# Small tensors of a low-rank gate: loaded by another engine, prepared two products sooner

## The chip, the cores and the metric

The kernel runs on one core of one Trainium2 chip. Its time is the device time of one execution, in microseconds (us); a kernel is given by the median of several executions. The core has TensorE (PE in the profile: matrix products, with PEld for its weight loads), VectorE (DVE), ScalarE (ACT), GpSimd (POOL) and SyncE (SP, which in this kernel only issues DMAs). Each engine takes its instructions strictly in the order in which they were written down for it; an instruction that waits for a semaphore holds up all behind it on its engine.

## The reference

One layer of a hybrid decoder, 1024 tokens of width 1024, all in float32:

```python
h = rms_norm(x, pre_g)
z = einsum('bsd,de->bse', h, w_in)
qa, ka, va, ga, qb, kb, vb, gb, gk_low = split_columns(z)
...                                   # differential attention on qa, ka, va, gated by ga
gk = einsum('bsr,re->bse', gk_low, w_gk_up) + b_gk
log_a = log_sigmoid(gk) / 16
ob = gla_chunked(qb, kb, vb, log_a)   # gated linear attention
...
y = einsum('bse,ed->bsd', concatenate([oa, ob]), w_out)
return x + rms_norm(y, post_g)
```

The part that matters here is the low-rank gate: gk_low is a product of h with only 16 columns of w_in (a "low rank" of 16), and w_gk_up (16 x 512) widens it to the 512 gate values.

## The kernel before, in words

**Products.** The wide product h @ w_in is made by Strassen's method in Winograd's form: h and w_in are cut into 2 x 2 blocks, and seven block products replace eight. In the code a product is a pair (p, n): p a group of 256 columns of w_in (the list `pairs`; 0 to 3 are the values of the linear attention, 4 is the first of the attention's keys), n the number of the product, 1 to 7. The left factors are blocks or sums of blocks of h: h11, h12, h22, s1 to s4 (`LEFT`); the right ones blocks or differences of blocks of w_in. `order` lists all products in the order in which PE makes them. Around the change it runs: (0,5) (1,5) (0,6) (1,6) (0,4) (0,7) (1,4) (1,7), the first half of the low-rank product, (2,5), its second half, (3,5), (0,3) and so on. For pairs 0 to 3 one set of prepared weights serves both pairs of a couple: the weights of (0,6) are also those of (1,6).

**High and low parts.** To keep float32's precision, each factor is split into a high part, rounded to PE's fast format (fp32r), and a low part, the rest. A product is three matmul passes: high x high, high left x low weights, low left x high weights. So each weight costs a subtraction that forms the block difference (DVE, `w_raw<-w_raw`), a rounding (ACT, `CAST w<-w_raw`) and a second subtraction for the low part (DVE, `w<-w_raw,w`). The function `parts` does the same for a block of h: high part by ACT (`s_hi`, `h_hi`), low part by DVE (`s_lo`, `h_lo`); it returns the low part's instruction.

**Order of the work.** `go(n)` makes the next n products. Before product i it calls `prepare` for i to i + 3, and `make_weights` then writes down the operations of those weights and the loads of raw weights (`load_raw`, on SP). PE's order is that of the program, fixed by hand. The other engines' order comes from a planner that runs a model of the timeline while the kernel is built: whenever an engine comes free in the model, it takes the ready instruction that stands first in the program. So an instruction that the program names early has a higher rank, but one of lower rank that is ready earlier fills a hole. `tc.issue_after(ins)` adds an edge: the instructions within it that are for the engine of `ins` come behind `ins` in that engine's order.

**Blocks of h.** `blocks(j)`, for j = 0 to 3, transposes the lower rows of h, makes h21, h22 and the sums s1 = h21 + h22, s3 = h11 - h21 and s2 = s1 - h11, and splits them with `parts`. It returns the low parts of s2 and s3; after the last call they are in `behind`. They are used twice: `prepare` puts the weights of (0,4) behind the low part of s2 (L290), and the four sums s4 come behind both.

**Low-rank product.** `low_rank` (L783) clears `keep`, loads w_gk_up (16 x 512) into `gk_up` and the 16 columns of w_in into `wl` (1024 rows of 16 values, 64 bytes each), both by `sp.dma_start` (L790, L794), clears `wl2`, `gkl` and `up`, and then has DVE make, from `wl`, the block difference `wd`, and the high and low parts of both in `wl2`; and from `gk_up` the high and low parts in `up`. Then come `go(2)`, which is (1,4) and (1,7), and the two halves of the low-rank product, 16 matmuls each (`gkl_ps`): first the high, then the low parts of h against `wl2`. `gk_up`, `wl` with `wd`, and the tiles c, s1, h21 of other steps share a ring of four buffers, `t_c`. In the profile `wl2` is shown as wl, `up` and `keep` as ku.

Of the kernel before, what the change touches and what calls it, by code (L numbers as in the profile page):

```python
# [18 lines left out]
KT = D // P  # L19
HB = 4  # L20
# [5 lines left out]
QA, KA, VA, GA, QB, KB, VB, GB, GKL = 0, 1024, 2048, 3072, 4096, 4608, 5120, 6144, 7168  # L26
GK_RANK = 16
# [4 lines left out]
def hymba_kernel(  # L32
# [21 lines left out]
    pe, sp = nc.tensor, nc.sync  # L54
# [80 lines left out]
    def take_bank(shape, name):  # L135
        i = free.pop(0)
        return bank(i, shape, name), i
# [6 lines left out]
    def tr(dst, src):  # L144
        tc.keep_in_program_order(pe.transpose(dst, src, ident))  # L145
# [8 lines left out]
    def block(n):  # L154
        if n not in H:
            pool_h, pieces = (hpool, 1) if n in ("s3", "s4") else (hw, 2)
            H[n] = [
                [
                    pool_h.tile(
                        [P, HB // pieces, 512], F32R, tag=f"{n}_{part}{i}", name=f"{n}_{part}"  # L160
                    )
                    for i in range(pieces)
                ]
                for part in ("hi", "lo")
            ]
# [9 lines left out]
    kp = ctx.enter_context(tc.tile_pool(name="kp", bufs=1))  # L175
# [67 lines left out]
    order = [(0, 1), (1, 1), (0, 2), (1, 2), (2, 1), (3, 1), (2, 2), (3, 2), (4, 1), (4, 2)]  # L243
# [16 lines left out]
    i = order.index((1, 4))  # L260
# [22 lines left out]
    def prepare(i):  # L283

        if i >= len(order) or i in ws:
            return
        if 4 <= i <= n_early + 1:
            with tc.issue_after(act.last), tc.issue_after(dve.last):
                make_weights(i)
        elif order[i] == (0, 4):  # L290
            with tc.issue_after(behind[0].ins):
                make_weights(i)
        else:
            make_weights(i)
# [44 lines left out]
    def make_weights(i):  # L339
        p, n = order[i]  # L340
        if (wide(p) and p % 2) or p == VALS[1]:
            ws[i] = ws_wide[p - 1, n]
            return
        if p in VALS:
            ws[i] = ws_wide[p, n] = value_weights(n)
            return
        if p in early and n < 3:
            src = early[p][n - 1]
        else:
            fetch_raw(p, n, i)  # L350
# [12 lines left out]
            if n == 5:  # L363
                src = sub(b11, b12, b11)
            elif n == 6:
                src = sub(b11, b22, b11)
            elif n == 4:
                src = sub(b21, b21, b11)
            elif n == 7:
                src = sub(b12, b22, b12)  # L370
            else:
                src = {1: b11, 2: b21, 3: b22}[n]
        if wide(p):
            w = [ap.tile([P, HB, 256], F32R, tag="ring", name="w", bufs=NRING) for _ in range(2)]
# [299 lines left out]
    def parts(n, j, f):  # L674
        hi, lo = block(n)
        act.copy(at(hi, j), f)
        return dve.tensor_tensor(at(lo, j), f, fp(at(hi, j)), ALU.subtract)

    def blocks(j):


        pss = []
        for k in (j, j + HB):
            ps, i = take_bank([P, 512], "xT")
            for n in range(4):
# [12 lines left out]
        parts("h22", j, h22)  # L698
        parts("s1", j, s1)
        h11 = f1[0][:, j]  # L700
        dve.tensor_tensor(h21, h11, h21, ALU.subtract)
        dve.tensor_tensor(h11, s1, h11, ALU.subtract)
        return [parts("s2", j, h11), parts("s3", j, h21)]

    made = [0]
    fill = []
# [32 lines left out]
    def go(n):  # L739
        for _ in range(n):  # L740
            i = made[0]
            if i == len(order):
                return
            made[0] = i + 1
            for a in range(4):
                prepare(i + a)
            step(i)
            if order[i][0] >= EARLY and order[i][0] not in VALS:
                wo_step(order[i][1])
            for _ in range(2 if order[i][0] in VALS else 1):  # L750
                if fill and next(fill[0], 0) == 0:
                    fill.pop(0)
# [11 lines left out]
    for j in range(HB):  # L764
        behind = blocks(j)
# [14 lines left out]
    ku = kp.tile([P, 2, 512], F32R, tag="ks1", name="ku")  # L780
    up, keep = ku[:, 0], fp(ku)[:, 1]

    def low_rank():  # L783


        R = GK_RANK
        pool.memset(keep, 1.0)
        pool.memset(keep.rearrange("p (c i) -> p c i", i=64)[:, :, 0:1], 0.0)
        gk_up = t_c("gk_up")[:R]
        sp.dma_start(gk_up, w_gk_up[0])  # L790
        wl2 = kp.tile([P, KT + HB, 64], F32R, tag="q0", name="wl2")
        wd = t_c("wd").rearrange("p (k r) -> p k r", r=R)
        wd, wl = wd[:, KT : KT + HB], wd[:, :KT]
        sp.dma_start(wl, w_in[0, :, GKL : GKL + GK_RANK].rearrange("(k p) c -> p k c", p=P))  # L794
        pool.memset(fp(wl2), 0.0)
        dve.tensor_tensor(wd, wl[:, HB:], wl[:, :HB], ALU.subtract)
        for dst, src in ((wl2[:, :KT], wl), (wl2[:, KT:], wd)):
            dve.tensor_copy(dst[:, :, :R], src)
            dve.tensor_tensor(dst[:, :, 32 : 32 + R], src, fp(dst[:, :, :R]), ALU.subtract)
        pool.memset(fp(gkl), 0.0)  # L800
        pool.memset(fp(up), 0.0)
        dve.tensor_copy(up[0:R], gk_up)
        dve.tensor_copy(up[32 : 32 + R], gk_up)
        dve.tensor_tensor(up[64 : 64 + R], gk_up, fp(up[0:R]), ALU.subtract)
        dve.tensor_tensor(up[96 : 96 + R], gk_up, fp(up[0:R]), ALU.subtract)
        go(2)
        for half in range(2):
            cs = cols(half)
            ps, i = take_bank([P, 512], "gkl_ps")
            terms = ((0, "h11"), (HB, "h12")) if half == 0 else ((0, "s1"), (KT, "h22"))  # L810
            for part in range(2):
                for o, n in terms:
                    for k in range(HB):
                        mm(
                            ps[:64], wl2[:, o + k, :], at(H[n][part], k),
                            start=(part == 0 and o == 0 and k == 0),
                            stop=(part == 1 and o != 0 and k == HB - 1),
                        )
            free.append(i)
            low = t_c("low")[:R]  # L820
            act.copy(low, ps[32 : 32 + R])
            dve.tensor_tensor(low, low, ps[:R], ALU.add)
            dve.tensor_copy(gkl[0:R, cs], low)
            dve.tensor_copy(gkl[64 : 64 + R, cs], low)
            dve.tensor_tensor(gkl[32 : 32 + R, cs], low, fp(gkl[0:R, cs]), ALU.subtract)
            dve.tensor_tensor(gkl[96 : 96 + R, cs], low, fp(gkl[0:R, cs]), ALU.subtract)
            go(1)

    def decay(g):
# [27 lines left out]
        act.activation(b, b, AF.Exp, scale=1.0 / 16)  # L857
        decs[g] = b, t

    go(4)  # L860
    sp.dma_start(bgk, b_gk[0].rearrange("(t p) -> p t", p=P))
    low_rank()
# [814 lines left out]
```

## Time and profile before

| | |
|---|---|
| median of three runs | 976.76 us |
| the three runs | 976.76, 975.23, 977.49 us |
| the profiled execution | 977.06 us |
| its span, first to last instruction | 975.4 us |
| mean granted clock of PE | 0.997 |
| busy: PE, DVE, ACT, POOL | 960.7, 736.2, 604.3, 203.3 us |

The profile is that of one execution. Its time lies 1.7 us above its span. A row of a timeline has the start in us from the span's begin, the length in us (of several like instructions together), the engine (SPq is SP's queue), the line, the operation, what it writes and reads, and how many instructions; in brackets the idle time of the engine before it and whose end ended it. L66 is the helper through which most operations go, L142 the matmul helper, so a row is known by its tiles. A row of the waits names who waited for whom: us in total, how often, the longest. A row of the windows gives the stretch and then, for each engine, its busy time; PEclk is the clock that PE was granted, 1.00 being full speed.

### The profile page before, as it was taken

The page shows a single profiled execution, that of the slowest core. Times are in us where ns is not written, and L with a number is a line of the kernel's source. Part 1 is how long each engine was busy: PE and PEld are TensorE (multiplying, and loading weights), DVE is VectorE, ACT ScalarE, POOL GpSimd, SP SyncE. Part 2 cuts the span into 40 slices and gives each one's busy share as a digit, 9 for nine tenths or more (in the row PEclk, how much of TensorE's full clock was granted, in tenths as well). Part 3 has the DMA queues.
Part 4 walks back from the last instruction along what each step waited for, and adds up shares of the span by engine and source line. Part 5 has one row for each costly group of instructions (what it writes and reads, how often), then busy time and mean ns, then how long its engine had stood idle before and what let it go on. Part 6 is the DMA issues. An engine that isn't in the chain of part 4 may idle for free.

```text
span 975.4 us, 15092 instructions
## 1 busy us (share of the span) xinstructions
PE 960.7 (98%) x4977; PEld 815.6 (84%) x4977; DVE 736.2 (75%) x1464; ACT 604.3 (62%) x1166; POOL 203.3 (21%) x264
## 2 busy tenths in 40 slices
PE   9998999999999999999999999999999999999997
PEld 7997988888888888888888888878888888888785
DVE  5996598997677686686766576587888888898555
ACT  8741354664766555576765344366786777887773
POOL 4300001222141221221100002121322222443322
PEclk9999999999999999999999999999999999999999
DMA  9442357468668987996764589997656669994777
GB/s 359 149 124 76 119 152 253 163 224 302 219 195 259 279 278 264 286 285 216 249 190 146 167 245 283 390 289 244 225 177 218 234 198 349 327 297 104 152 206 149
DMA packets 152302, 220.39 MB, mean 226 GB/s; under 512 B 16753, under 2 KB 87409, under 8 KB 152129
## 3 DMA queue, kind: packets, MB, share of 16 engines
q1 hardware_dynamic: 138128, 178.80, 57.3%
q0 software_dynamic: 14096, 40.64, 14.4%
q8 instruction: 39, 0.64, 0.3%
q14 instruction: 39, 0.31, 0.1%
HBM read 133.93 MB, written 88.60 MB: 228 GB/s over the span
## 4 chain that ended last, share of the span: by engine, by line
PE 88%; DVE 4%; DMA 4%; SPq 2%; issue 2%; ACT 1%; POOL 0%; DVEq 0%; ACTq 0%; POOLq 0%
PE x L142 22%; PE z L142 15%; PE y L142 14%; PE ypart L142 12%; PE sc L142 6%; PE po L142 5%; PE yps L142 4%; PE wtr L145 3%; PE gpo L142 3%; PE kv L142 1%; DMA w_early<-in_w_in_dram 1%; PE gkl_ps L142 1%; DVE p L66 1%; DMA mixd<-gate 1%; PE pa L142 1%
## 5 line engine op out<-in xcount | busy, mean ns | idle before, releaser
L66 ACT CAST w<-w_raw 128x512 fp32r<-128x512 f32 (+1 forms) x150 | 98.0, 655 | 90.5 <-PE y L142 46.3
L66 DVE TENSOR_TENSOR w<-w_raw,w 128x512 fp32r<-128x512 f32 (+1 forms) x150 | 109.3, 731 | 50.4 <-ACT w L66 46.2
L66 ACT ACTIVATE p<-p,stt 128x896 f32<-128x896 f32 (+7 forms) x128 | 99.3, 777 | 36.2 <-DVE stt L66 35.2
L66 ACT COPY s<-x 128x512 f32<-128x512 f32 x82 | 47.7, 586 | 92.5 <-PE x L142 92.0
L66 POOL TENSOR_SCALAR p<-p,stt,lam 128x1024 f32<-128x1024 f32 (+3 forms) x64 | 56.0, 874 | 148.4 <-DVE stt L66 146.6
L66 POOL DMA_DIRECT2D wo_d<-wo_hi x32 | 17.6, 550 | 331.3 <-ACT wo_hi L66 331.3
L66 DVE CUSTOM_DVE_ANT_0 p<-sc,maskt 128x512 f32<-128x512 f32 (+3 forms) x128 | 74.2, 585 | 14.3 <-PE sc L142 13.1
L142 PE MATMUL z<-s_hi,w 128*128 128x512 f32 x320 | 80.2, 393 | 0.0
L142 PE MATMUL x<-s_hi,w 128*128 128x512 f32 x320 | 80.1, 392 | 0.0
L142 PE MATMUL y<-h_hi,w 128*128 128x512 f32 x320 | 80.0, 392 | 0.0
L142 PE MATMUL ypart<-wo_hi,m_hi 128*128 128x512 f32 x192 | 79.5, 414 | 0.1
L142 PE MATMUL ypart<-wo_hi,m_lo 128*128 128x512 f32 x192 | 75.5, 393 | 0.0
L142 PE MATMUL ypart<-wo_lo,m_hi 128*128 128x512 f32 x192 | 75.4, 393 | 0.0
L142 PE MATMUL sc<-k,q 128*128 128x512 f32 (+1 forms) x192 | 69.1, 363 | 1.7 <-DVE stt L66 1.7
L142 PEld LDWEIGHTS y<-h_hi,w 128*128 128x128 f32 x320 | 59.7, 188 | 12.3
L142 PEld LDWEIGHTS z<-s_hi,w 128*128 128x128 f32 x320 | 59.7, 188 | 12.3
L142 PEld LDWEIGHTS x<-s_hi,w 128*128 128x128 f32 x320 | 59.7, 188 | 12.3
L66 DVE TENSOR_TENSOR w_raw<-w_raw 128x512 f32<-128x512 f32 (+1 forms) x88 | 66.1, 751 | 3.3 <-DMA w_raw<-in_w_in_dram 2.2
L142 PE MATMUL sc<-ks,q 128*128 128x512 f32 (+1 forms) x192 | 66.1, 347 | 0.0
L66 ACT CAST wt_hi<-wtr 128x512 fp32r<-128x512 f32 (+1 forms) x80 | 42.7, 534 | 25.7 <-PE wtr L145 24.9
L66 DVE TENSOR_TENSOR wt_lo<-wtr,wt_hi 128x512 fp32r<-128x512 f32 (+1 forms) x80 | 50.6, 632 | 9.5 <-ACT wt_hi L66 8.8
L66 DVE TENSOR_TENSOR c<-z,s 128x512 f32<-128x512 f32 x48 | 32.9, 688 | 31.4 <-ACT s L66 18.3
(223 smaller groups left out, 2350.0 us busy)
## 6 DMA issues: line engine op xcount, KB each, us to landing
w_raw<-in_w_in_dram SPq DMA_DIRECT2D x48, 512.0 KB, 4.8
wo_d<-wo_hi POOLq DMA_DIRECT2D x32, 256.0 KB, 3.8
q<-q_d SPq DMA_DIRECT2D x32, 256.0 KB, 5.2
k<-k_d SPq DMA_DIRECT2D x32, 256.0 KB, 5.8
ks<-k_d SPq DMA_DIRECT2D x64, 128.0 KB, 6.2
v<-v_d SPq DMA_DIRECT2D x16, 512.0 KB, 7.7
wo_raw<-in_w_out_dram POOLq DMA_DIRECT2D x31, 256.0 KB, 4.9
wo_d<-gqd POOLq DMA_DIRECT2D x22, 256.0 KB, 4.3
```

The lines of the kernel that those rows point to most:

```text
L66: ins = op(*a, **k)
L142: tc.keep_in_program_order(pe.matmul(*a, **k))
L145: tc.keep_in_program_order(pe.transpose(dst, src, ident))
```

## The change

Two edits that are apart from each other, and a third that serves the first.

1. The low-rank gate's preparation becomes a function of its own, `low_rank_weights`. It is called after products (0,6) and (1,6), two products sooner in the program than before, and `low_rank` keeps only the two halves of the product. PE's order stays as it was: the two calls `go(2)` and `go(4)` cover the six products that `go(4)` and the inner `go(2)` covered.
2. Its two loads are issued by POOL, not SP; its DVE operations stand behind `behind[0]`, the low part of s2 of the last block.
3. `blocks` also returns the low part of s1, and the weights of (0,6) stand behind it (`behind[2]`). Before, only those of (0,4) stood behind anything.

```diff
@@ -287,8 +287,8 @@
-        elif order[i] == (0, 4):
-            with tc.issue_after(behind[0].ins):
+        elif order[i] in ((0, 6), (0, 4)):
+            with tc.issue_after(behind[2 if order[i] == (0, 6) else 0].ins):
                 make_weights(i)
@@ -696,11 +696,11 @@
-        parts("s1", j, s1)
+        s1_lo = parts("s1", j, s1)
...
-        return [parts("s2", j, h11), parts("s3", j, h21)]
+        return [parts("s2", j, h11), parts("s3", j, h21), s1_lo]
@@ -780,30 +780,33 @@
-    def low_rank():
-
-
-        R = GK_RANK
+    wl2 = kp.tile([P, KT + HB, 64], F32R, tag="q0", name="wl2")
+    R = GK_RANK
+
+    def low_rank_weights():
+
         pool.memset(keep, 1.0)
         pool.memset(keep.rearrange("p (c i) -> p c i", i=64)[:, :, 0:1], 0.0)
         gk_up = t_c("gk_up")[:R]
-        sp.dma_start(gk_up, w_gk_up[0])
-        wl2 = kp.tile([P, KT + HB, 64], F32R, tag="q0", name="wl2")
+        pool.dma_start(gk_up, w_gk_up[0])
         wd = t_c("wd").rearrange("p (k r) -> p k r", r=R)
         wd, wl = wd[:, KT : KT + HB], wd[:, :KT]
-        sp.dma_start(wl, w_in[0, :, GKL : GKL + GK_RANK].rearrange("(k p) c -> p k c", p=P))
+        pool.dma_start(wl, w_in[0, :, GKL : GKL + GK_RANK].rearrange("(k p) c -> p k c", p=P))
         pool.memset(fp(wl2), 0.0)
-        dve.tensor_tensor(wd, wl[:, HB:], wl[:, :HB], ALU.subtract)
-        for dst, src in ((wl2[:, :KT], wl), (wl2[:, KT:], wd)):
-            dve.tensor_copy(dst[:, :, :R], src)
-            dve.tensor_tensor(dst[:, :, 32 : 32 + R], src, fp(dst[:, :, :R]), ALU.subtract)
         pool.memset(fp(gkl), 0.0)
         pool.memset(fp(up), 0.0)
-        dve.tensor_copy(up[0:R], gk_up)
...
-        go(2)
+        with tc.issue_after(behind[0].ins):
+            dve.tensor_tensor(wd, wl[:, HB:], wl[:, :HB], ALU.subtract)
+            for dst, src in ((wl2[:, :KT], wl), (wl2[:, KT:], wd)):
+                dve.tensor_copy(dst[:, :, :R], src)
+                dve.tensor_tensor(dst[:, :, 32 : 32 + R], src, fp(dst[:, :, :R]), ALU.subtract)
+            dve.tensor_copy(up[0:R], gk_up)
...
+
+    def low_rank():
+
         for half in range(2):
@@ -857,6 +860,8 @@
+    go(2)
+    low_rank_weights()
     go(4)
     sp.dma_start(bgk, b_gk[0].rearrange("(t p) -> p t", p=P))
     low_rank()
```

More of the change, by code (lines that the diff above doesn't have):

```diff
@@ L789, in low_rank @@
         gk_up = t_c("gk_up")[:R]
-        sp.dma_start(gk_up, w_gk_up[0])
-        wl2 = kp.tile([P, KT + HB, 64], F32R, tag="q0", name="wl2")
+        pool.dma_start(gk_up, w_gk_up[0])
         wd = t_c("wd").rearrange("p (k r) -> p k r", r=R)
         wd, wl = wd[:, KT : KT + HB], wd[:, :KT]
-        sp.dma_start(wl, w_in[0, :, GKL : GKL + GK_RANK].rearrange("(k p) c -> p k c", p=P))
+        pool.dma_start(wl, w_in[0, :, GKL : GKL + GK_RANK].rearrange("(k p) c -> p k c", p=P))
         pool.memset(fp(wl2), 0.0)
-        dve.tensor_tensor(wd, wl[:, HB:], wl[:, :HB], ALU.subtract)
-        for dst, src in ((wl2[:, :KT], wl), (wl2[:, KT:], wd)):
-            dve.tensor_copy(dst[:, :, :R], src)
-            dve.tensor_tensor(dst[:, :, 32 : 32 + R], src, fp(dst[:, :, :R]), ALU.subtract)
         pool.memset(fp(gkl), 0.0)
         pool.memset(fp(up), 0.0)
-        dve.tensor_copy(up[0:R], gk_up)
-        dve.tensor_copy(up[32 : 32 + R], gk_up)
-        dve.tensor_tensor(up[64 : 64 + R], gk_up, fp(up[0:R]), ALU.subtract)
-        dve.tensor_tensor(up[96 : 96 + R], gk_up, fp(up[0:R]), ALU.subtract)
-        go(2)
+        with tc.issue_after(behind[0].ins):
[4 more added lines that the diff above has]
+            dve.tensor_copy(up[0:R], gk_up)
+            dve.tensor_copy(up[32 : 32 + R], gk_up)
+            dve.tensor_tensor(up[64 : 64 + R], gk_up, fp(up[0:R]), ALU.subtract)
+            dve.tensor_tensor(up[96 : 96 + R], gk_up, fp(up[0:R]), ALU.subtract)
+    def low_rank():
         for half in range(2):
```

## The prediction

> **What bounds the kernel now.** I read the page first, for which engine sets the time; then the list of what TensorE (PE) waited for; then the timeline of PE, to place these waits; then those of DVE, ACT and SP around them.
>
> ```profile
> PE 960.7 (98%) x4977; PEld 815.6 (84%) x4977; DVE 736.2 (75%) x1464; ACT 604.3 (62%) x1166; POOL 203.3 (21%) x264
> ...
> PE gkl_ps L142 <- DVE wl L66: 2.7, 1, 2.7
> PE z L142 <- DVE s_lo L66: 0.5, 1, 0.5
> ```
>
> PE is busy for 960.7 of 975.4 us, so only its few waits can be won. The two lines are both in the stage that the diff touches. PE's timeline there (start, length, idle time before it and who ended it):
>
> ```profile
> 52.87 0.50 PE L142 MATMUL z<-w,s_lo 128*128 128x256 f32 x2 [0.51 <-DVE s_lo L66]
> ...
> 56.09 2.08 PE L142 MATMUL x<-w,s_hi 128*128 128x256 f32 x16
> ...
> 61.85 2.08 PE L142 MATMUL y<-w,h_hi 128*128 128x256 f32 x16
> ...
> 72.41 1.12 PE L142 MATMUL x<-w,s_lo 128*128 128x256 f32 x8
> 76.27 3.27 PE L142 MATMUL gkl_ps<-h_hi,wl 128*64 128x512 f32 x8 [2.74 <-DVE wl L66]
> ...
> 81.22 2.08 PE L142 MATMUL z<-w,s_hi 128*128 128x256 f32 x16
> ...
> 84.09 1.07 PE L142 MATMUL gkl_ps<-s_hi,wl 128*64 128x512 f32 x4
> ...
> 87.76 2.08 PE L142 MATMUL z<-w,s_hi 128*128 128x256 f32 x16
> ```
>
> PE stood still for 0.51 us before 52.87, in the product (0, 5), which lacked the last low part of the sum s1; and for 2.74 us before 76.27, because the low-rank weights `wl2` (shown as wl) were not ready. The second stall costs more than its length. The 16 matmuls of the first low-rank half run from 76.27 to 81.22, 4.95 us; the 16 of the second, the same shapes, from 84.09 to 87.76, 3.67 us. The granted clock says why:
>
> ```profile
> 73.50:76.20 2.70, 0.03 (x1) 0.00 (x0) 2.70 (x5) 1.63 (x2) 0.00 (x0) 0.88 0.00 0
> 76.20:77.50 1.30, 1.24 (x3) 0.73 (x4) 1.30 (x3) 0.00 (x0) 0.00 (x0) 0.50 0.31 34
> ```
>
> The clock was at 0.50 right after the idle stretch: 4.95 - 3.67 = 1.28 us. So the two places hold 0.51 + 2.74 + 1.28 = 4.53 us, 0.46% of the span.
>
> The Trainium skill's page "TensorE: Matmul & The Clock Gate" (Part 1: The HAM clock gate) has the clock fall to half after an idle window of about 3.4 us; taken strictly, 2.74 us of idling would not do it, and the sum would lack the 1.28. The trace shows the drop after 2.74 us, and the trace decides.
>
> **Why wl was late.** It is no long operation; it stands at the end of two queues. SP's and DVE's rows:
>
> ```profile
> 58.72 5.05 SPq L220 DMA_DIRECT2D w_raw<-in_w_in_dram  x3
> 63.82 0.50 SPq L790 DMA_DIRECT2D gk_up<-in_w_gk_up_dram  x1
> 64.38 0.41 SPq L794 DMA_DIRECT2D wd<-in_w_in_dram  x1
> ...
> wd<-in_w_in_dram SPq DMA_DIRECT2D x1, 64.0 KB, 4.4
> ```
>
> ```profile
> 50.40 1.21 DVE L66 TENSOR_TENSOR w_raw<-w_raw 128x1024 f32<-128x1024 f32 x1
> 51.54 0.68 DVE L66 TENSOR_TENSOR h<-f1hi,h 128x512 f32<-128x512 f32 x1
> 52.14 0.68 DVE L66 TENSOR_TENSOR s_lo<-s,s_hi 128x512 fp32r<-128x512 f32 x1
> ...
> 54.54 1.21 DVE L66 TENSOR_TENSOR w<-w_raw,w 128x1024 fp32r<-128x1024 f32 x1
> ...
> 56.88 0.68 DVE L66 TENSOR_TENSOR s_lo<-f1hi,s_hi 128x512 fp32r<-128x512 f32 x1
> 57.49 1.21 DVE L66 TENSOR_TENSOR w_raw<-w_raw 128x1024 f32<-128x1024 f32 x1
> 58.62 2.48 DVE L66 TENSOR_TENSOR s<-f1lo,f1hi 128x512 f32<-128x512 f32 x4
> 61.03 2.34 DVE L66 TENSOR_TENSOR w<-w_raw,w 128x1024 fp32r<-128x1024 f32 x2
> 63.30 1.21 DVE L66 TENSOR_TENSOR w_raw<-w_raw 128x1024 f32<-128x1024 f32 x1
> ...
> 69.63 0.85 DVE L66 CAST ku<-gk_up 16x512 fp32r<-16x512 f32 x2
> ...
> 71.66 0.22 DVE L66 TENSOR_TENSOR wd<-wd 128x64 f32<-128x64 f32 x1
> 71.79 0.22 DVE L66 CAST wl<-wd 128x128 fp32r<-128x128 f32 x1
> 72.04 1.38 DVE L66 TENSOR_TENSOR ku<-gk_up,ku 16x512 fp32r<-16x512 f32 x2
> 73.45 1.22 DVE L66 TENSOR_TENSOR w_raw<-w_raw 128x1024 f32<-128x1024 f32 x1
> 74.60 0.19 DVE L66 CAST wl<-wd 128x64 fp32r<-128x64 f32 x1
> 74.70 1.22 DVE L66 TENSOR_TENSOR w<-w_raw,w 128x1024 fp32r<-128x1024 f32 x1
> 75.83 0.28 DVE L66 TENSOR_TENSOR wl<-wd,wl 128x128 fp32r<-128x128 f32 x1
> ...
> 78.37 0.22 DVE L66 TENSOR_TENSOR wl<-wd,wl 128x64 fp32r<-128x64 f32 x1
> ```
>
> SP runs in order: both small loads stand behind three w_raw loads, which themselves wait for buffers that DVE frees. They go out at 63.82 and 64.38 and land 4.4 us later, at 68.8. DVE takes them from 69.63 on, mixed with two large operations (73.45, 74.70) that PE needs only much later. The low part of wl ends at 75.83 + 0.28 = 76.11, and PE starts at 76.27.
>
> **The change, part by part.**
>
> *Low-rank part.* Nothing is added or removed: the same DVE operations, 0.85 + 0.22 + 0.22 + 1.38 + 0.19 + 0.28 + 0.22 = 3.36 us, the same memsets, the same two loads. They enter the program two products earlier, ahead of what the products (0, 4) and (0, 7) set off, so the planner ranks them above the gv_st sums, the subtractions and the weights of 63.30 to 74.70. Their floor is the new edge: not before the low part of s2, which ends at 56.88 + 0.68 = 57.56. Above them still rank the four s4 sums (58.62) and the weights of (0, 4) and (0, 7) (61.03), to 63.37. If all 3.36 us then run at one go, they end at 66.7. PE comes to the low-rank product at 72.41 + 1.12 = 73.53, or 73.0 with the first stall gone: 6.3 us of room. Slipping by up to that costs nothing; beyond it each us costs one, and the clock with it. The bounds of the gain are 0 and 4.02. I take the whole 2.74 + 1.28 as won.
>
> The loads on POOL's queue: POOL has only memsets there, and nothing later stands behind the loads until the output weights.
>
> ```profile
> 40.38 0.96 POOL L66 MEMSET gkl<- 128x1024 f32 x1 [1.89 <-DVE w L66]
> ...
> L66 POOL DMA_DIRECT2D wo_raw<-in_w_out_dram x31 | 17.1, 552 | 0.3 <-issue 0.3
> wo_raw<-in_w_out_dram POOLq DMA_DIRECT2D x31, 256.0 KB, 4.9
> ```
>
> A POOL load of 128 runs of 2 KB takes 0.55 us to issue and lands 4.9 us later. The wl load is 1024 runs of 64 bytes, which no POOL row shows. Bounds on its issue: 0.55 us (like the row) and 8 x 0.55 = 4.4 us (if it goes by runs). Its buffer, one of four in the ring "c", is free by about 57 (the last block's s1 and h21 tiles are read before the row of 56.88 starts). So it lands between 57 + 0.55 + 4.9 = 62.5 and 66.3. I take the near end, the row's own figure; at the far end wl is done by 66.3 + 3.4 = 69.7, still 3.3 us early. SP loses two issues (0.50 + 0.41 us) in a stretch in which it only waits for DVE: nothing won.
>
> What is displaced: 63.30 and its followers begin up to 3.4 us later, but DVE's total is the same, so all is done by 76 as before. The first that PE needs of it is the weights of (2, 5), in before at 81.22, after the change near 76.7. The next wait of the low-rank product itself would be its PSUM bank, given back by ACT's copy after (0, 7), two products ahead: covered.
>
> *Sixth weights.* Now the subtraction of (0, 6) (50.40, 1.21 us) stands before s1's low part (52.14). Put behind it, it lets h (51.54) and the low part move up by 1.14 us; the low part ends at 52.82 - 1.14 = 51.68, before PE's need at 52.87 - 0.51 = 52.36: 0.51 won. The price is that (0, 6) itself becomes late:
>
> ```profile
> 51.65 1.05 ACT L66 CAST w<-w_raw 128x1024 fp32r<-128x1024 f32 x1 [0.71 <-DVE w_raw L66]
> ...
> 59.65 2.00 ACT L66 CAST w<-w_raw 128x1024 fp32r<-128x1024 f32 x2
> ```
>
> Its high part (1.05, now 51.65) follows the subtraction, its low part (54.54) the high one. PE would want the high part at 56.09 - 0.51 = 55.58, the low one 1.04 us later (half of the 2.08 us) at 56.62. If the subtraction takes the place just behind the low part (51.68 to 52.85), both are in time: cost nothing. If the planner puts two more sums of 0.60 before it, the high part ends at 55.1, the low part at 56.3: in time. With three more, 55.7 and 56.9: late by 0.3. Bounds 0 to 0.5 (then nothing is won). I take 0.2, near the placement just behind.
>
> (0, 4) is near its bound too: its low part ends at 61.03 + 1.21 = 62.24 and PE, 0.51 earlier, wants it at 61.34 + 1.04 = 62.38. 0.14 us is left: nothing by the sum, and the first place to break.
>
> **Sum.** 2.74 + 1.28 + 0.51 - 0.2 = 4.3 us. Besides these two and its first instruction, the list of PE's waits names only groups of the attention (sc, po, wtr), far behind, so by the profile nothing near takes it back. The profiled execution took 977.06 us (span 975.4 and 1.7 around it), so 972.8; it lies 0.3 above the median of the runs, 976.76. Against the median: **972.5 us**.
>
> **Rivals.**
> 1. *The stall moves to (0, 4).* The planner fills low-rank work in ahead of the low part of (0, 4). For: 0.14 us of room, 3.36 us of work. Against: it ranks lower, and (0, 4)'s high part (59.65 + 1.05) ends before the s4 sums do (61.10), so DVE has no hole to fill. Part of it (the 0.85 of ku and the 0.44 of wd and wl): a stall of 1.2 us, gain 3.1, 973.7. All of it: a stall of 3.2 and the clock's 1.28, 4.5 against the 4.3 won: 977.0, no change.
> 2. *Slower: DVE blocked by the POOL load.* DVE runs in order. If the planner counts on an early landing and puts the wl operations right behind 57.49 (end 58.70), DVE stands there until the load lands, with the s4 sums and (0, 4)'s weights behind. At the late landing, 66.3, DVE loses 7.6 us; (0, 4)'s low part comes at 62.24 + 7.6 + 0.66 = 70.5 against 62.38: 8.1 us of stall and 1.28 of clock against 4.3 won, so +5.1: 981.9. In that order it decides from a landing after 61.2 on (then 3.0 of stall and 1.28 of clock eat the 4.3). For: the run count. Against: the s4 sums rank higher, so the first place for wl is 63.37. The Trainium skill's page "SBUF — State Buffer" (SBUF: two separate sides, "The 'DVE blocks DMA' trap") speaks for a late landing: descriptors that GpSimd writes are held up while DVE runs certain copies. But DVE's rows from 50.40 to 63.30 are two-input operations, which that page (Who interferes with whom) sets apart from the copies.
> 3. *The edits do nothing*: wl still last in DVE's order. 976.3, for the 0.51 alone. The rank argues against it.
>
> **Chances.** Forecast (gain 3.5 to 5) 0.66; the partial form of rival 1 (gain 2 to 3.5) 0.11; rival 1 whole or rival 3 (no change) 0.12; rival 2, or another order of DVE elsewhere with the same sign, 0.11. A measurement of this kernel can tell about 0.2%, 1.95 us, from no change: faster 0.77, same 0.12, slower 0.11. Range: below, the full 4.53 and the 1 us by which such medians wander (runs of before 975.23 to 977.49), 971.2; above, past the partial cases and into the no-change ones, 976.0.
>
> **What would show it.** In PE's waits the lines for gkl_ps and z are gone or under 0.2 us; the first low-rank half takes 3.7 us at clock 1.00; DVE's wl rows lie between 60 and 70; the two loads are POOL rows and land before 67. Wrong if: a new wait of PE for w at (0, 6) or (0, 4), wl rows still after 73, a DVE gap that ends with the landing of wd, or a new gap after 81.

## The result and the profile after

| | before | changed |
|---|---|---|
| median | 977.23 us | 973.21 us |
| executions, lowest to highest | 6, 975.23 to 978.39 us | 6, 972.67 to 973.52 us |
| profiled execution, its span | 977.06, 975.4 us | 972.82, 971.1 us |
| PE busy | 960.7 us | 958.7 us |

The ratio is 0.996, with a 95% interval of 0.9947 to 0.9973: faster by 4.0 us, 0.4%.

What PE waited for in the changed kernel (us in total, how often, the longest): the two largest groups, spin with 1.5 us and sc with 1.3, lie at the kernel's start and in the attention. The third lies in the stage that the change touches:

```profile
PE y L142 <- DVE w L66: 1.0, 1, 1.0
```

Both lines of before that the prediction rested on, gkl_ps with 2.7 us and z with 0.5, are gone. A line has come in their place: 1.0 us of y, a product whose weights DVE had not finished. PE's timeline places it:

```profile
49.71 2.08 PE L142 MATMUL z<-w,s_hi 128*128 128x256 f32 x16
51.62 1.12 PE L142 MATMUL z<-w,s_lo 128*128 128x256 f32 x8
...
55.46 2.30 PE L142 MATMUL x<-w,s_hi 128*128 128x256 f32 x16
...
61.44 1.12 PE L142 MATMUL y<-w,h_hi 128*128 128x256 f32 x8
63.60 1.21 PE L142 MATMUL y<-w,h_hi 128*128 128x256 f32 x8 [1.04 <-DVE w L66]
...
74.24 2.00 PE L142 MATMUL gkl_ps<-h_hi,wl 128*64 128x512 f32 x8
...
77.91 2.08 PE L142 MATMUL z<-w,s_hi 128*128 128x256 f32 x16
```

The second row is the low pass of (0,5) without a break. The row of 55.46, (0,6), lasts 2.30 us where the other high passes take 2.08: 0.22 lost inside it, at the low part of its weights, which DVE ended at 56.48 (55.27 + 1.21) and PE came to at 56.42 (55.46 + 0.96). (0,4) is broken in two, and its second half, the high left factor on the low weights, begins 1.04 us late. The first low-rank half, 74.24 to 77.91, takes 3.67 us, as the second one did before. The windows' PEclk column (the third number from the end) agrees; these are the stretches of the changed kernel in which before had no PE work (0.88) and then a clock of 0.50:

```profile
73.50:76.20 2.70, 2.70 (x17) 1.94 (x16) 2.70 (x4) 0.77 (x2) 0.00 (x0) 1.00 0.45 134
76.20:77.50 1.30, 1.30 (x8) 0.72 (x7) 1.30 (x3) 0.87 (x1) 0.00 (x0) 1.00 0.89 273
```

DVE's and POOL's rows show what moved, and what made (0,4) late. DVE first, then the ACT row that holds the high parts of (0,4) and (0,7):

```profile
51.13 0.68 DVE L66 TENSOR_TENSOR s_lo<-s,s_hi 128x512 fp32r<-128x512 f32 x1
51.73 1.21 DVE L66 TENSOR_TENSOR w_raw<-w_raw 128x1024 f32<-128x1024 f32 x1
...
58.75 2.49 DVE L66 TENSOR_TENSOR s<-f1lo,f1hi 128x512 f32<-128x512 f32 x4
61.16 0.86 DVE L66 CAST ku<-gk_up 16x512 fp32r<-16x512 f32 x2
62.05 0.23 DVE L66 TENSOR_TENSOR wd<-wd 128x64 f32<-128x64 f32 x1
62.19 0.22 DVE L66 CAST wl<-wd 128x128 fp32r<-128x128 f32 x1
62.32 2.35 DVE L66 TENSOR_TENSOR w<-w_raw,w 128x1024 fp32r<-128x1024 f32 x2
...
65.84 1.38 DVE L66 TENSOR_TENSOR ku<-gk_up,ku 16x512 fp32r<-16x512 f32 x2
...
67.37 0.28 DVE L66 TENSOR_TENSOR wl<-wd,wl 128x128 fp32r<-128x128 f32 x1
```

```profile
59.24 2.00 ACT L66 CAST w<-w_raw 128x1024 fp32r<-128x1024 f32 x2
```

The row of 51.73 is the subtraction for (0,6), now directly behind the low part of s1 (51.13). The ku, wd and wl rows of 61.16 to 62.41 are low-rank work, 1.25 us of it, **ahead of** the row of 62.32, whose first half is the low part of (0,4)'s weights. The low part of wl, which ended at 76.11 before, ends at 67.37 + 0.28 = 67.65. The weights' high part can't have been what DVE waited for: ACT had it at 59.24 + 1.05, about 60.3. Now POOL, and the landing times of the two loads:

```profile
50.92 0.73 POOL L66 DMA_DIRECT2D gk_up<-in_w_gk_up_dram  x1 [9.45 <-DVE s_lo L66]
55.37 0.98 POOL L66 DMA_DIRECT2D wd<-in_w_in_dram  x1 [3.72 <-DVE s_lo L66]
```

```profile
wd<-in_w_in_dram POOLq DMA_DIRECT2D x1, 64.0 KB, 3.0
gk_up<-in_w_gk_up_dram POOLq DMA_DIRECT2D x1, 32.0 KB, 2.2
```

### The profile page after: what moved, and what is told of

The parts are those of the page before. It is cut to its first block, busy times and chain, and to the rows that moved or that the text cites. A ratio compares the mean times of both kernels' runs of the same rounds, so it can differ in the third digit from the quotient of the medians.

```text
span 971.1 us, 15096 instructions
## 1 busy us (share of the span) xinstructions
PE 958.7 (99%) x4977; PEld 814.5 (84%) x4977; DVE 735.5 (76%) x1464; ACT 604.6 (62%) x1166; POOL 207.9 (21%) x266
## 4 chain that ended last, share of the span: by engine, by line
PE 94%; ACT 3%; DVE 1%; issue 1%; DMA 0%; POOL 0%; DVEq 0%; ACTq 0%; POOLq 0%
PE x L142 23%; PE z L142 16%; PE y L142 16%; PE ypart L142 13%; PE sc L142 7%; PE po L142 5%; PE yps L142 4%; PE wtr L145 3%; PE gpo L142 3%; PE kv L142 1%; ACT junk L66 1%; PE gkl_ps L142 1%; PE pa L142 1%; DVE p L66 1%; ACT h_hi L66 0%
```

## Where the 4 us come from

PE's program is the same in both kernels, so the distance from the start of (0,5) to later products compares them free of what came earlier. In us, worked out from the starts in PE's timelines, as in 76.27 - 49.57 = 26.70:

| from the start of (0,5) to | before (49.57) | changed (49.71) | won so far |
|---|---|---|---|
| (0,4) | 12.28 | 11.73 | 0.55 |
| the low-rank product | 26.70 | 24.53 | 2.17 |
| (2,5) | 31.65 | 28.20 | 3.45 |

"The second edit" is from here on number 3 of the list of the change: the weights of (0,6) behind the low part of s1. It makes the first line. A break in PE's work costs more than its idle time: 0.16 us, since a matmul of 256 columns lasts 0.28 us but the next follows 0.12 behind it when none waits, and about 0.1 more in the matmuls right behind it (eight of them take 1.21 us after the new wait, 1.12 elsewhere). So 0.51 of idle and 0.26 of the break are 0.77 won up to (0,6), less the 0.22 in (0,6). In the second line, 2.90 us at the low-rank product are won (2.74 of idle and 0.16), and 1.29 are lost again to the new wait (1.04, 0.16 and 0.09). The third line adds the clock: 4.95 less 3.67 is 1.28.

The stage gives 3.45 us. The profiled spans differ by 4.3. The other 0.8 lies outside the stage: 0.36 at the very end and 0.6 in the attention, of which more below, less the 0.14 by which (0,5) began later.

## The experiments

All were compared with before on the same chip; before's median was 976.81, 976.82 and 976.90 us in the three groups of runs. "Stage" is the distance from the start of (0,5) to the start of (2,5) in the profiled execution: 31.65 us before, 28.20 in the changed kernel.

| run | median, range, executions | ratio to before, 95% | stage |
|---|---|---|---|
| e0_changed_again | 973.11, 972.94 to 973.40, 5 | 0.9961, 0.9947 to 0.9974 | 28.23 |
| e4_lowrank_behind_07 | 971.24, 970.83 to 972.07, 5 | 0.9943, 0.9930 to 0.9955 | 27.06 |
| e3_loads_by_sp | 973.23, 973.08 to 973.94, 4 | 0.9964, 0.9950 to 0.9977 | 28.24 |
| e2_lowrank_without_sixth | 973.26, 972.64 to 974.50, 4 | 0.9964, 0.9951 to 0.9978 | 28.23 |
| e1_sixth_only | 976.56, 974.94 to 977.87, 10 | 1.0000, 0.9991 to 1.0009 | 30.00 |
| e7_behind_07_without_sixth | 972.66, 971.18 to 973.40, 5 | 0.9958, 0.9944 to 0.9971 | 27.47 |
| e5_warm_matmuls | 974.89, 974.38 to 975.80, 10 | 0.9985, 0.9976 to 0.9994 | 30.37 |
| e6_loads_early_only | 974.07, 973.82 to 975.43, 10 | 0.9975, 0.9966 to 0.9984 | 30.21 |
| e8_ranked_early_loads_late | 973.44, 972.33 to 974.08, 5 | 0.9962, 0.9948 to 0.9976 | 27.69 |

### The changed kernel again

No edit; the yardstick for its group.

> The changed kernel once more, as the measure for the others. The stage between the sixth weights and the product (2,5) is set by fixed orders, so PE should again reach (2,5) at 77.9 us (81.2 before), with a wait of about 1.0 us in (0,4) and none at the low-rank product. The rest of the gain, 0.8 of the 4.0 us, lay behind that stage (a wait for sc in the attention and the tail): if it is part of the change it comes back, if it is the spread of single executions these two places differ by some tenths. Time 973.2, ratio 0.995 to 0.997.

Time, stage and the wait of y (1.0 us) came out as in the first profile.

### Low-rank work behind (0,7)'s weights

Does the low-rank work ahead of (0,4)'s low part make the new wait, or are (0,4)'s weights late by themselves, because PE reaches them 0.5 us sooner? The edge is moved, so that the work can't get ahead:

```diff
+    lows = {}
...
-        dve.tensor_tensor(w[1], src, fp(w[0]), ALU.subtract)
+        lows[p, n] = dve.tensor_tensor(w[1], src, fp(w[0]), ALU.subtract)
...
-        with tc.issue_after(behind[0].ins):
+        with tc.issue_after(lows[0, 7].ins):
```

> The changed kernel with one edge moved: the low-rank DVE operations stand behind the low part of the weights of (0,7), not behind the low part of s2. Theory: the new wait in (0,4) is the 1.3 us of low-rank work (ku 0.86, wd and wl 0.45) that DVE does ahead of the low weights; without it the low part of (0,4) ends near 62.4, the wait falls from 1.04 to under 0.2 us, PE reaches (2,5) near 76.7 instead of 77.9, the low-rank weights are still ready before 73, and the time is 1.2 us less than the changed kernel's, about 972.0. Rival: the low weights are late for a reason of their own (ACT's high part, buffers); then the wait stays above 0.5 us and the time is the same. Second rival: the low-rank weights now come too late, and the wait at the low-rank product is back.

DVE, then PE, of this run:

```profile
61.42 2.35 DVE L66 TENSOR_TENSOR w<-w_raw,w 128x1024 fp32r<-128x1024 f32 x2
63.69 0.21 DVE L66 TENSOR_TENSOR wd<-wd 128x64 f32<-128x64 f32 x1
...
67.90 0.28 DVE L66 TENSOR_TENSOR wl<-wd,wl 128x128 fp32r<-128x128 f32 x1
```

```profile
61.70 2.20 PE L142 MATMUL y<-w,h_hi 128*128 128x256 f32 x16
...
73.33 1.99 PE L142 MATMUL gkl_ps<-h_hi,wl 128*64 128x512 f32 x8
...
77.00 2.08 PE L142 MATMUL z<-w,s_hi 128*128 128x256 f32 x16
```

The weights of (0,4) and (0,7) now come first, (0,4) runs through in one row, and the low part of wl (67.90) still comes 5 us before its use at 73.33. The stage is 1.17 us shorter: the new wait with its break, 1.29, less 0.12 that (0,4) still loses (2.20 us against 2.08). So the low-rank work made the wait, and (0,4) is late by itself by those 0.12 alone. The median is 1.9 us below that of the changed kernel on the same chip, 0.7 more than the stage gives; in the profiles 0.5 of it lies in the attention, and it isn't explained. This version beats both kernels: no execution of it was as long as the shortest of the other two.

### The loads by SP

Does the engine that issues the loads matter, or only where they stand?

```diff
-        pool.dma_start(gk_up, w_gk_up[0])
+        sp.dma_start(gk_up, w_gk_up[0])
...
-        pool.dma_start(wl, w_in[0, :, GKL : GKL + GK_RANK].rearrange("(k p) c -> p k c", p=P))
+        sp.dma_start(wl, w_in[0, :, GKL : GKL + GK_RANK].rearrange("(k p) c -> p k c", p=P))
```

> The changed kernel with its two small loads issued by SP again, at their new place in the program. DVE's order is the same as in the changed kernel. Theory: what helps is that the loads go out before the three w_raw loads, not which engine issues them; SP gets them at about 51 and 55 us, they land by 60, PE reaches (2,5) at 77.9 as in the changed kernel, time 973.2 within 1. Rival: SP must wait for the buffer of wl (about 55 us) and holds up what stands behind it, or the loads land after 62; then DVE stands still before wd, (0,4) waits longer than 1.04 us, and (2,5) comes after 78.5.

SP's row of the wl load in this run, and its landing time:

```profile
55.97 0.54 SPq L794 DMA_DIRECT2D wd<-in_w_in_dram  x1
```

```profile
wd<-in_w_in_dram SPq DMA_DIRECT2D x1, 64.0 KB, 2.7
```

The wl load goes out 0.6 us later than POOL's and lands within 0.3 us of it (55.97 + 2.7 against 55.37 + 3.0). DVE's order was the same, the wait of y too (1.05), the stage 28.24. At their new place in the program the loads don't stand behind the three w_raw loads; SP would have done as well.

### Without the second edit

Do the two gains add, or does (0,4), which waits for DVE anyway, take back what the second edit wins?

```diff
-        elif order[i] in ((0, 6), (0, 4)):
-            with tc.issue_after(behind[2 if order[i] == (0, 6) else 0].ins):
+        elif order[i] == (0, 4):
+            with tc.issue_after(behind[0].ins):
```

> The changed kernel without its second edit: the weights of (0,6) stand behind nothing, as before. Theory that the two stalls add up: the wait of 0.51 us for the last low part of s1 is back, (2,5) comes 0.5 to 0.7 us later, near 78.5, time 973.8. Rival: between the two places DVE, not PE, sets the end (the low part of (0,4) ends at 63.5 whatever PE does), so the 0.51 us at s1 only shorten the wait in (0,4), from 1.04 to about 0.5, and (2,5) stays at 77.9; the second edit is worth nothing here. I hold the rival the likelier.

PE's timeline of this run:

```profile
53.03 0.50 PE L142 MATMUL z<-w,s_lo 128*128 128x256 f32 x2 [0.52 <-DVE s_lo L66]
...
63.63 1.22 PE L142 MATMUL y<-w,h_hi 128*128 128x256 f32 x8 [0.50 <-DVE w L66]
...
77.95 2.08 PE L142 MATMUL z<-w,s_hi 128*128 128x256 f32 x16
```

The wait of 0.52 in (0,5) is back, and that of (0,4) has shrunk from 1.04 to 0.50. (0,4)'s second half begins at 63.63, with the edit at 63.60, and the stage and the time are the same: nothing adds, since DVE fixes this point.

### The second edit alone

The kernel before with this part of the change and nothing else:

```diff
-        elif order[i] == (0, 4):
-            with tc.issue_after(behind[0].ins):
+        elif order[i] in ((0, 6), (0, 4)):
+            with tc.issue_after(behind[2 if order[i] == (0, 6) else 0].ins):
...
-        parts("s1", j, s1)
+        s1_lo = parts("s1", j, s1)
...
-        return [parts("s2", j, h11), parts("s3", j, h21)]
+        return [parts("s2", j, h11), parts("s3", j, h21), s1_lo]
```

> The kernel before with the second edit alone: the weights of (0,6) behind the last low part of s1, the low-rank part as before. If the stalls add up, the wait of 0.51 us at s1 goes and the time falls by 0.5 to 0.7 us. If DVE's order sets the end of the stage, the wait at s1 goes, but the low-rank weights are ready at the same time as before, so PE waits there about 3.3 us instead of 2.74, reaches (2,5) at the same distance from (0,5) as before (31.65 us), and the time is that of before. I expect the second.

PE in the profiled execution, and the windows around the stall (PEclk third from the end):

```profile
49.92 2.08 PE L142 MATMUL z<-w,s_hi 128*128 128x256 f32 x16
...
72.36 1.12 PE L142 MATMUL x<-w,s_lo 128*128 128x256 f32 x8
76.22 2.04 PE L142 MATMUL gkl_ps<-h_hi,wl 128*64 128x512 f32 x8 [2.74 <-DVE wl L66]
...
79.92 2.08 PE L142 MATMUL z<-w,s_hi 128*128 128x256 f32 x16
```

```profile
73.40:76.20 2.80, 0.07 (x1) 0.01 (x1) 2.79 (x5) 1.63 (x2) 0.00 (x0) 1.00 0.00 0
76.20:77.50 1.30, 1.28 (x6) 0.82 (x7) 1.30 (x3) 0.00 (x0) 0.00 (x0) 1.00 0.30 29
```

The low-rank product began at 76.22, against 76.27 before, but in this execution (0,5) itself began 0.35 us later (49.92 against 49.57). By the distance from (0,5) the low-rank product comes at 26.30 us instead of 26.70: 0.40 of the edit are won, and PE waits 2.74 us as before, not the 3.3 expected. DVE does set this time, but in the kernel before it had waited for PE on the way. DVE's same operation in before, then in this run:

```profile
68.42 0.69 DVE L66 TENSOR_TENSOR gv_st<-z,s 128x512 f32<-128x512 f32 x1 [0.37 <-ACT s L66]
```

```profile
68.38 0.69 DVE L66 TENSOR_TENSOR gv_st<-z,s 128x512 f32<-128x512 f32 x1
```

In before DVE stood for 0.37 us until ACT had copied out (0,7), which ACT in turn had from PE; with PE 0.4 us earlier this wait is gone, and all behind it on DVE comes sooner. The median can't tell: its ratio of 1.0, with 0.9991 to 1.0009, leaves room for 0.4 us either way.

The clock is the surprise, and makes the other 1.25 of the 1.65 us by which this stage is shorter. PE stood still for 2.74 us as before, and this time the clock stayed at 1.00; the first half took 3.70 us (76.22 to 79.92), not 4.95. Of the ten executions three took 974.94 (the profiled one) to 975.53 us and seven 976.46 to 977.87: as if the same idle time sometimes costs the clock and sometimes not. Before's 50 executions over all groups fall apart likewise, 11 from 974.98 to 976.02 us and 39 from 976.57 up, while the changed kernel's 11 keep within 0.9 us. Only two of these executions have windows to look at. For the others there is the mean granted clock of the whole execution; 3.4 us at half (the windows of before have it low from 75.55 to about 78.97) lower it by about 0.002. Of the executions of these two kernels whose clock is on record, 31 of 54 have 0.997 or less; of those of the kernels without the 2.74 us of idle time, none of 54. All 31 are among the longer ones. But 10 of before's 34 longer executions there have 0.998 or 0.999, like the short ones, so the time alone doesn't show whether the clock fell.

### The edge at (0,7) without the second edit

Does the second edit pay once DVE no longer sets the end?

```diff
-        elif order[i] in ((0, 6), (0, 4)):
-            with tc.issue_after(behind[2 if order[i] == (0, 6) else 0].ins):
+        elif order[i] == (0, 4):
+            with tc.issue_after(behind[0].ins):
...
-        with tc.issue_after(behind[0].ins):
+        with tc.issue_after(lows[0, 7].ins):
```

> The kernel with the low-rank work behind the weights of (0,7), but without the second edit: the weights of (0,6) free again. With the wait in (0,4) gone, DVE is no longer late there, so the wait at s1 should now cost its full length: (2,5) 27.6 to 27.7 us after (0,5), against 27.1 with the second edit, time 971.8. Rival: it is worth nothing here either (27.1, 971.2).

The stage is 27.47 us, 0.41 above that with the second edit. So the edit is worth 0.4 us in the stage when nothing behind it waits. The medians differ by 1.4 us across two groups of runs on different chips; the other 1.0 isn't in the stage (in the two profiles the attention differs by 1.7).

### Warm matmuls in the stall

Is the 1.28 us really the clock's? Eleven matmuls of h11 with ones go into the low-rank product's bank ahead of its first half, which overwrites them; the wait for wl stays.

```diff
+            if half == 0:
+                for _ in range(11):
+                    mm(ps, ones, at(H["h11"][0], 0), start=True, stop=True)
```

> The kernel before with eleven more matmuls (ones against h11, into the low-rank product's own bank, which the product then overwrites) just ahead of the first low-rank half, so that PE works through most of its wait for the low-rank weights; nothing else is changed, and no result of the product. About 11 x 0.23 = 2.5 us of work in a wait of 2.74. Theory: the slow first half (4.95 us against 3.67) is the clock that fell while PE stood still; with PE at work it stays at 1.00, the first half takes 3.7 us, (2,5) comes 1.28 us earlier, time 1.3 us less than before. Rival: the first half is slow for another reason (its operands, the weights just written); then it still takes 4.9 us and the time is that of before or a little longer.

PE and the windows of this run:

```profile
73.43 2.71 PE L142 MATMUL gkl_ps<-h_hi,ones 128*128 128x512 f32 x11
76.33 2.02 PE L142 MATMUL gkl_ps<-h_hi,wl 128*64 128x512 f32 x8 [0.19 <-DVE wl L66]
...
80.02 2.08 PE L142 MATMUL z<-w,s_hi 128*128 128x256 f32 x16
```

```profile
76.20:77.50 1.30, 1.17 (x6) 0.73 (x7) 1.30 (x3) 0.00 (x0) 0.00 (x0) 1.00 0.23 25
```

The low-rank product begins no earlier (76.33), but its first half takes 3.69 us at a clock of 1.00, and the stage is 31.65 - 30.37 = 1.28 us shorter. The median falls by 1.9 us, and the ratio's interval, 0.9976 to 0.9994, has room for the 1.28. One profile at 1.00 would prove little, since the clock sometimes holds without the matmuls too. But none of the ten executions has a mean clock below 0.998, where 14 of 27 of before in the same group have 0.997 or less, and none is longer than 975.80 us. So PE's idle time is what lowered the clock, and where it falls the price is the 1.28 us of the prediction. The median's other 0.6 us aren't explained.

### The loads early, the DVE work at its old place

Is it the rank of the DVE work, its place in the program, that moves it up? Or the loads, so that the planner fills the work in as soon as the data are there? Here the loads are at their new place on POOL and the second edit is in, but the DVE work stands at its old place, without an edge.

```diff
     def low_rank_weights():
...
+        return gk_up, wl, wd
...
     def low_rank():
+        gk_up, wl, wd = loads
         dve.tensor_tensor(wd, wl[:, HB:], wl[:, :HB], ALU.subtract)
...
+    go(2)
+    loads = low_rank_weights()
+    go(2)
```

> The changed kernel with the low-rank DVE work back at its old place in the program, behind no edge, while the two loads stay early and on POOL. Theory of rank (that of the prediction): DVE's low-rank work ranks low again, is done between 69 and 76, and the wait at the low-rank product comes back, (2,5) near 81. Theory of readiness: the planner takes what is ready when it has a hole, so early data alone pull the work forward; with no edge to hold it back it comes even before the low weights of (0,6) and (0,4) (ku's 0.86 and 1.38 us more than in the changed kernel), the wait at the low-rank product is gone, but (0,6) and (0,4) wait about 2 us more together, and (2,5) comes near 79.5: a time of 974.5 to 975.

DVE, then PE, of this run:

```profile
55.38 1.29 DVE L66 CAST ku<-gk_up 16x512 fp32r<-16x512 f32 x2
56.70 1.23 DVE L66 TENSOR_TENSOR w<-w_raw,w 128x1024 fp32r<-128x1024 f32 x1
...
62.71 1.38 DVE L66 TENSOR_TENSOR ku<-gk_up,ku 16x512 fp32r<-16x512 f32 x2
...
64.40 2.36 DVE L66 TENSOR_TENSOR w<-w_raw,w 128x1024 fp32r<-128x1024 f32 x2
```

```profile
57.98 1.21 PE L142 MATMUL x<-w,s_hi 128*128 128x256 f32 x8 [1.32 <-DVE w L66]
...
65.67 1.22 PE L142 MATMUL y<-w,h_hi 128*128 128x256 f32 x8 [1.68 <-DVE w L66]
...
76.33 2.00 PE L142 MATMUL gkl_ps<-h_hi,wl 128*64 128x512 f32 x8
```

The stage is 30.21 us, as expected; the median, 974.07, lies below the 974.5 to 975 expected, and the attention was short here (291.5 us). The wait at the low-rank product is gone, although the DVE work stands late in the program: the loads alone suffice for that. Without the edge to `behind[0]` the work goes even further ahead: a ku cast in front of (0,6)'s low part (56.70), the ku, wd and wl operations from 62.71 on in front of (0,4)'s (64.40). PE waits 1.32 and 1.68 us there. So the edge of the change seems to have a use after all, to keep the work behind (0,6)'s weights; rank and edge were both taken away here, and no run takes the edge alone.

The ku casts hold a second lesson. The row of 55.38 has two of them; the first took 0.41 us, and the second, begun at 55.82 while POOL issued the wl load (55.47 to 56.45), 0.86, against 0.42 in each of the other ten profiles. The load landed after 3.0 us as elsewhere. So beside the load's issue it was DVE's copy that was slow, not the load; it happened once, and the cause wasn't tested.

### Ranked early, the loads late

The converse: the DVE work early in the program, with its edge, and both loads on SP behind the second of the three w_raw loads (`raw_load` holds what `load_raw` issues).

```diff
-        pool.dma_start(gk_up, w_gk_up[0])
+        with tc.issue_after(raw_load[3, 1].ins):
+            sp.dma_start(gk_up, w_gk_up[0])
...
-        pool.dma_start(wl, w_in[0, :, GKL : GKL + GK_RANK].rearrange("(k p) c -> p k c", p=P))
+        with tc.issue_after(raw_load[3, 1].ins):
+            sp.dma_start(wl, w_in[0, :, GKL : GKL + GK_RANK].rearrange("(k p) c -> p k c", p=P))
```

> The converse of the run with the loads alone: the low-rank DVE work stays at its early place in the program (with its edge, and with the second edit), but both loads are issued by SP behind the second of the three w_raw loads, at about 63 us, nearly as late as before. If early data are what the change needs, the data land at 67 to 69, the low-rank weights are late again (after 75) and PE reaches (2,5) more than 31 us after (0,5). If the early place in the program is enough, DVE takes the data soon after they land, the weights are ready at about 73.5, PE waits 0.3 to 0.8 us for them, nothing of the low-rank work stands before the low weights of (0,4), so that wait is gone, and (2,5) comes 27.5 to 27.9 us after (0,5), sooner than in the changed kernel (28.2). Time about 972.8. I expect the second.

SP, DVE, then PE, of this run:

```profile
63.45 0.41 SPq L796 DMA_DIRECT2D wd<-in_w_in_dram  x1
63.96 0.53 SPq L220 DMA_DIRECT2D w_raw<-in_w_in_dram  x1
```

```profile
68.15 0.86 DVE L66 CAST ku<-gk_up 16x512 fp32r<-16x512 f32 x2
...
73.28 0.29 DVE L66 TENSOR_TENSOR wl<-wd,wl 128x128 fp32r<-128x128 f32 x1
```

```profile
61.49 2.22 PE L142 MATMUL y<-w,h_hi 128*128 128x256 f32 x16
...
73.71 2.04 PE L142 MATMUL gkl_ps<-h_hi,wl 128*64 128x512 f32 x8 [0.41 <-DVE wl L66]
```

With data that come late nothing can get ahead of (0,4): no wait there, and 0.41 us at the low-rank product. The stage is 27.69 us, 0.5 better than the changed kernel's. So early loads alone take the stall of 2.74 us away, and bring the wait at (0,4) with them; the early rank leaves 0.41 of it. The rank doesn't do this quite alone: the wl load goes out at 63.45 and lands after 3.3 us, at 66.8, 2 us sooner than in before. Of the 2.5 us by which the low part of wl ends sooner (73.57 against 76.11), 1.1 lie behind the first ku cast, where DVE mixes in fewer large operations, which fits the rank. The 1.5 ahead of that cast can be the loads' as well; no run separates them. The median is no lower than the changed kernel's (973.44); in the profile the attention was 1.3 us longer and the end 0.36.

### The end of the kernel, and what stays open

The last stores are issued at 971.43 us in before and 967.56 in the changed kernel; the spans end 4.0 and 3.5 us later. SP closes the program with a series of ten waits on its DMA semaphores, in a fixed order, which pass 0.06 us apart when nothing holds them. From PE's end to the span's end it is 6.63 us in all five profiles whose two loads are on SP (before, e1, e3, e5, e8) and 6.25 to 6.27 in all six whose loads are on POOL. In before the last store uses the second semaphore of the series, in the changed kernel the last. Two loads fewer on SP shift which store has which semaphore, and e3, which differs from the changed kernel in these two lines alone, has 6.63. So 0.36 us of the profile's gain have nothing to do with the stage; that the semaphores' order makes them is read from the records and not tested by itself, and the medians of e3 and the changed kernel, 973.23 and 973.11, are too close to show it.

The attention, from its first scores to the first output product, took 293.1 us before, 292.5 in the changed kernel, and 291.5 to 293.8 in the experiments. It isn't touched by the edits, but the planner orders all engines anew for each kernel. Two profiles of the changed kernel have 292.5 and 292.3, so chance alone made 0.2 there; more was not separated. The second edit alone and the warm matmuls, neither near the attention, have 292.2 and 292.1, so the 0.6 us need not come from the change. They, and the 0.7 that e4 has beyond its stage, stay open.

## Why the prediction was right, and where it wasn't

- **The wait for wl, 2.74 us, and the clock, 1.28: right.** Both are gone from the trace. The warm matmuls show the clock's share by itself, 1.28 us. It isn't paid in each execution: with the second edit alone an idle time of the same 2.74 us left the clock at 1.00. The page "TensorE: Matmul & The Clock Gate" of the Trainium skill (Part 1: The HAM clock gate) calls the clock's window free-running; that fits a stall that costs the clock in one execution and not in another. The page's idle window of about 3.4 us was not needed here: in before the stretch from 73.50 to 76.20 has a mean of 0.88, so 0.12 x 2.70 / 0.5 = 0.65 us of it were at half, and the drop came 2.0 us after PE stopped. Nothing here shows where the chip's window began in either execution.
- **The step that failed: "0.14 us is left: nothing by the sum, and the first place to break".** It broke. The new wait at (0,4) is one of the prediction's own signs of being wrong, and the partial form of rival 1 (its chance was 0.11) came true, about as priced: 0.86 of ku and 0.45 of wd and wl ahead of (0,4)'s low part, 1.3 us lost (1.04 of idle and 0.25 of the break). It moved the forecast's 4.3 to 3.45 in the stage, and would have taken more, had the sum not also left out the 0.42 us that the two breaks cost besides their idle time. That the profiled execution still took the 972.8 us of the sum (972.82) is luck: the 0.8 us outside the stage, which the sum did not have, made up for it. The medians came the same way, 4.0 us apart where 4.3 were forecast. The argument against the rival was that DVE has no hole: (0,4)'s high part ended before the s4 sums did. That was so on the chip too: ACT had it at about 60.3, and DVE took ku at 61.16. But the order is fixed by the planner's model, not by the chip. That the model had the high part later is the likely reason; the model's own times were not looked at.
- **"so the planner ranks them above the gv_st sums": incomplete.** With early loads the DVE work moves up at its old rank too: rank isn't needed for it. With late loads an early rank brings most of it, though there the data still came 2 us sooner than in before. What the prediction took for the effect of rank alone has two causes, of which the early loads suffice by themselves.
- **The second edit, 0.51 less 0.2: not additive.** It won 0.55 up to (0,4), and the wait there took it back; without it the kernel is as fast. Where (0,4) doesn't wait, it is worth 0.41, and in the kernel before 0.40. Its cost in (0,6) came out at 0.22 us against the 0.2 that was put in, but not by the working. The subtraction took the place just behind s1's low part, for which the working gave no cost; it let the low weights follow the high ones at once, and DVE put them behind four other operations, 0.06 us too late, and the break made it 0.22.
- **The loads.** Landing at 62.5 to 66.3 us was too late by far: 55.37 + 3.0 is 58.4. Taking the near end of the issue's bounds was right: 0.98 us, where the bounds were 0.55 and 4.4. The buffer was free before the 57 that I took: POOL's wait for it ends at 55.37. The earliness counted: it is what let the work get ahead of (0,4).
- **Rival 2, DVE blocked by the load:** no DVE row waits for wd. In the 3.0 us of the wl load DVE ran two-input operations, and nothing was held up, which agrees with the Trainium skill's page "SBUF — State Buffer" (Who interferes with whom). Under a copy, in the run with the loads alone, the load was no slower either; the copy was, by 0.44 us.

## What to carry to other kernels

A gain that is read as the sum of two waits need not add up: ask which engine's finish fixes the end of the stage. Time won ahead of that point is only spent waiting at it, unless that engine has itself waited for the faster one on the way, as DVE had in the kernel before. Where a planner orders the work, data that come early can do what a high rank does, and work that may run early gets ahead of what PE needs next: bind it behind the last thing that is urgent (here (0,7)'s weights, 1.2 us), not behind something earlier. And a stall on PE can cost more than its length: after 2.74 us the clock came back at half in one profile and at full speed in another.

## What the runs showed of the hardware

- The clock fell to half 2.0 us after PE stopped in one profile and not at all in a stop of the same 2.74 us in another; stops of 1.04, 1.32 and 1.68 us left it at 1.00. Once it had fallen it stayed low for 3.4 us (75.55 to about 78.97).
- A DMA of 1024 runs of 64 bytes took POOL 0.98 us to issue and 3.0 us to land, SP 0.54 and 2.7; 128 runs of 2 KB take 0.55 to issue on POOL and 16 runs of 2 KB took 0.73, so the cost doesn't go by the number of runs.
- A copy on DVE that ran while POOL issued a load took 0.86 us instead of 0.42, in the one case on record; the load took no longer.
- With the two loads on SP the kernel's end was 0.36 us longer, in five profiles against six; that the closing waits make it was not tested by itself.
